# Two more gate chunks as seven products; q and k normed in the recurrence and kept in DRAM; the first branch inside attention

## The chip, the core and the metric

The kernel runs on one core of a Trainium2 chip. The metric is device time in microseconds (us) of one whole execution. The core has a matrix engine, TensorE (PE; its weight loads are listed apart as PEld), and three others: VectorE (DVE), ScalarE (ACT) and GpSimd (POOL). SyncE (SP) issues most DMAs; ACT and POOL issue a few. Each engine runs its instructions in the order of the program and waits on semaphores for what others make.

## The reference

One layer over 1024 frames of width 1024, all in float32:

```
h = RMSNorm(x);  z = h @ w_in -> qa, fa, ia, ga, qb, kb, vb, gate_a, gate_b
oa = HGRN2(qa, fa, ia, ga)           # 4 heads of 128, chunk-causal recurrence
ob = BandAttn(head_rms(qb), head_rms(kb), vb)   # 8 heads of 64, own chunk of 64 and 8 before
x += (sigmoid(gate_a)*(oa @ w_branch_a) + sigmoid(gate_b)*(ob @ w_branch_b)) @ w_out
x += (silu(RMSNorm(x) @ w_gate) * (RMSNorm(x) @ w_up)) @ w_down
x += sigmoid(RMSNorm(x) @ w_ple_gate) * (p @ w_ple_proj)
```

The products hold float32 accuracy: each operand is split into a high part (cast to fp32r) and a rest, and a product of two operands is three matmuls (high by high, high by rest, rest by high).

## The kernel before

**Tiles and names.** A matmul is 128 rows by 128 columns of weights with 512 columns of data, written `128x512`; its result stands in one of eight PSUM banks (`pm`). A weight unit is 128x1024: a raw tile `wr` loaded by SP, its high part `wh` cast on ACT, its rest `wl = wr - wh` made on POOL or DVE. There are two raw tiles (RAW = 2) and four pairs of `wh`, `wl` (RING = 4), so the load of a unit waits until the rest of the unit two before it is made. Large tiles (128x1024) are `s`, small ones `m`; tiles in DRAM are `d`.

**Stages**, by the time in the profiled execution: the first norm and the products for gates, heads and outputs (0 to 284 us); the recurrence of four HGRN heads (about 304 to 437); band attention (447 to 640); the two branches with their gates; the output product; the FFN; the last gate. In the first stage, the table JOBS lists pairs of chunks made as seven half-size products over sums of halves (84 matmuls of 128x512 for a pair instead of 96).

**Recurrence.** `hgrn_mix` of a head begins with two sums over constants, passes levels m = 1, 2, 4, 8, 16, 32, 64 (a few matmuls, then a chain of DVE multiplications and ACT copies that the next level needs), transposes, and ends with eight steps of state. `weave` puts pieces of other work, the fill, between them, by a table of expected durations: the gate chunks of FIRSTS (four, 48 matmuls each), `attn_v`, and the first block of 128 frames of the q/k product. The fill is what PE does while a level's chain runs on DVE and ACT.

**Attention.** `attn_in` makes q and k for two halves of the heads (eight blocks each, four pieces of work per block, six matmuls a piece). A block is squared on ACT, summed on DVE, raised to the power -1/2 on POOL, and scaled on DVE into an SBUF tile. `attention` runs 34 steps; a step takes two pieces from the feed, and has scores, softmax, transposes and the product with v of up to five blocks. Weight rests are made by `rest()` on DVE from a queue, one or two a step, except those that `direct=True` sends to POOL. Late in the loop (steps 23, 25, 27, 28 of SPLITS) the four tiles of oa, loaded back from DRAM, are split into high part and rest on ACT and POOL.

**Branches.** `branches` then makes the eight chunks of the first branch from oa, multiplied by their gates, and the eight of the second from ob.

The helper lines matter when reading rows: L102 is the matmul, L105 the transpose, L97 the DMA that SP issues, L142 the cast of a weight unit, L150 its rest, L72 any other operation recorded through the ordering helper.

## Time and profile before

| | |
|---|---|
| median of three runs | 1539.81 us (1539.76 to 1542.86) |
| the profiled execution | 1538.44 us |
| span in its profile | 1536.7 us |
| mean granted clock of TensorE | 0.998 |
| PE busy | 1512.6 us, 98% of the span |
| DVE, ACT, POOL busy | 1106.7, 661.0, 643.2 us |
| 304.3 to 437 us: PE, DVE, ACT, POOL busy | 128.40, 102.47, 49.41, 19.06 of 132.70 us |
| 447 to 640 us: PE, DVE, ACT, POOL busy | 188.81, 133.22, 136.59, 69.91 of 193.00 us |

Rows of a group give line, engine, operation and tiles, the count, busy time, mean of one in ns, then the idle time of the engine ahead of them and what ended it. A row of the timeline gives the start, the length, and in brackets how long the engine had waited and for what. A row of a window gives its bounds, its length, then for each of PE, PEld, DVE, ACT, POOL the busy time with the count of instructions, then the granted clock, the share of the DMA engines and GB/s.

### The profile page before, as it was taken

The numbers are of one execution on the slowest core, as the hardware profiler recorded it, in microseconds if no ns is written. First come the engines' busy times: TensorE is split into PE (matmuls) and PEld (weight loads), VectorE is DVE, ScalarE is ACT, GpSimd is POOL, SyncE is SP. The second block draws the span as 40 slices with busy tenths as digits, with TensorE's granted clock in tenths as the row PEclk, the third lists the DMA queues.
The fourth block names the chain that finished last, engine by engine and source line by source line (L and its number), as shares of the span: only waits on it lengthen the run. The fifth ranks groups of instructions, "written<-read, shape, count | busy, mean of one in ns | idle before, by whom it ended". The sixth has DMA issues, their size and how long they took to land.

```text
span 1536.7 us, 20687 instructions
## 1 busy us (share of the span) xinstructions
PE 1512.6 (98%) x7692; PEld 1249.2 (81%) x7692; DVE 1106.7 (72%) x1599; ACT 661.0 (43%) x1109; POOL 643.2 (42%) x357
## 2 busy tenths in 40 slices
PE   8999999999999999999999999999999999999998
PEld 6888888888877877888888788888888888888886
DVE  5877776578766768447888877777777667756677
ACT  6633333434347768422575222222222234446452
POOL 4243333101132425254203666665555545545446
PEclk9999999999999999999999999999999999999999
DMA  5552444699553464676345344443333388875335
GB/s 210 189 171 83 144 144 144 219 318 326 179 144 56 98 169 144 189 223 201 123 162 183 114 118 125 123 126 107 103 103 103 103 322 307 282 271 178 124 102 200
DMA packets 97908, 258.66 MB, mean 168 GB/s; under 512 B 10128, under 2 KB 14992, under 8 KB 97296
## 3 DMA queue, kind: packets, MB, share of 16 engines
q1 hardware_dynamic: 91264, 241.60, 45.7%
q0 software_dynamic: 6400, 15.73, 6.1%
q8 instruction: 60, 0.98, 0.3%
q14 instruction: 40, 0.33, 0.1%
q10 hardware_dynamic: 144, 0.02, 0.0%
HBM read 194.13 MB, written 94.63 MB: 188 GB/s over the span
## 4 chain that ended last, share of the span: by engine, by line
PE 89%; DVE 5%; DMA 2%; ACT 2%; issue 1%; POOL 1%; SPq 0%; ACTq 0%; DVEq 0%; POOLq 0%
PE pm L102 86%; DVE s L72 4%; PE pm L105 2%; DMA wr<-in_wv 1%; DVE m L72 0%; ACT s L72 0%; ACT wh L142 0%; ACT m L72 0%; DMA wr<-in_fm 0%; DMA s<-in_x 0%; DVE q L72 0%; POOL m L72 0%; DVE s L337 0%; DVE t L72 0%; ACT t L72 0%
## 5 line engine op out<-in xcount | busy, mean ns | idle before, releaser
L102 PE MATMUL pm<-s,whi 128*128 128x512 f32 x1848 | 569.3, 389 | 0.6 <-DVE t L72 0.6
L102 PE MATMUL pm<-s,wh 128*128 128x512 f32 (+1 forms) x1520 | 472.1, 392 | 7.2 <-ACT wh L142 5.0
L102 PEld LDWEIGHTS pm<-s,whi 128*128 128x128 f32 x1848 | 346.6, 188 | 73.5 <-DVE t L72 1.6
L102 PE MATMUL pm<-s,wlo 128*128 128x512 f32 x924 | 359.5, 389 | 0.0
L102 PEld LDWEIGHTS pm<-s,wh 128*128 128x128 f32 x1520 | 284.3, 189 | 67.4 <-ACT wh L142 5.0
L72 DVE TENSOR_TENSOR s<-s,s 128x512 f32<-128x512 f32 (+3 forms) x236 | 285.6, 1239 | 51.2 <-ACT s L72 38.4
L102 PE MATMUL pm<-s,wl 128*128 128x512 f32 (+1 forms) x760 | 296.1, 390 | 0.5 <-POOL wl L150 0.5
L150 POOL TENSOR_TENSOR wl<-wr,wh 128x1024 fp32r<-128x1024 f32 (+2 forms) x72 | 175.8, 2446 | 220.3 <-ACT wh L142 216.1
L72 DVE TENSOR_TENSOR t<-pm,t 128x512 f32<-128x512 f32 x163 | 112.3, 689 | 139.3 <-PE pm L102 116.8
L102 PEld LDWEIGHTS pm<-s,wlo 128*128 128x128 f32 x924 | 173.5, 188 | 35.9
L142 ACT CAST wh<-wr 128x1024 fp32r<-128x1024 f32 (+2 forms) x104 | 104.5, 1005 | 204.4 <-PE pm L102 81.7
L102 PE MATMUL pm<-wh,s 128*128 128x512 f32 x512 | 180.7, 407 | 0.0
L102 PEld LDWEIGHTS pm<-s,wl 128*128 128x128 f32 x760 | 143.3, 189 | 30.7 <-POOL wl L150 1.2
L72 POOL TENSOR_TENSOR wlo<-q,whi 128x512 fp32r<-128x512 f32 x64 | 102.6, 1604 | 151.9 <-ACT whi L72 81.7
L72 POOL TENSOR_TENSOR wlo<-wr,whi 128x1024 fp32r<-128x1024 f32 (+1 forms) x65 | 136.0, 2098 | 68.8 <-ACT whi L72 59.8
L72 ACT CAST s<-s 128x1024 fp32r<-128x1024 f32 (+1 forms) x98 | 94.5, 983 | 57.8 <-DVE s L72 31.6
L72 ACT CAST whi<-q 128x512 fp32r<-128x512 f32 (+1 forms) x96 | 72.8, 758 | 107.4 <-PE pm L102 87.1
L72 POOL TENSOR_TENSOR m<-m,mhalf 128x8 f32<-128x8 f32 (+1 forms) x24 | 35.1, 1462 | 192.2 <-DVE m L72 192.1
L72 POOL TENSOR_TENSOR s<-t,rb 128x512 f32<-128x512 f32 x44 | 70.7, 1608 | 98.5 <-ACT t L72 98.5
L102 PEld LDWEIGHTS pm<-wh,s 128*128 128x128 f32 x512 | 96.3, 188 | 18.4
L102 PE MATMUL pm<-wl,s 128*128 128x512 f32 x256 | 100.0, 391 | 0.0
L72 ACT ACTIVATE t<-s 128x512 f32<-128x512 f32 x44 | 27.8, 633 | 159.3 <-DVE s L72 155.3
(151 smaller groups left out, 1769.1 us busy)
## 6 DMA issues: line engine op xcount, KB each, us to landing
s<-d SPq DMA_DIRECT2D x83, 512.0 KB, 6.5
d<-s SPq DMA_DIRECT2D x87, 256.0 KB, 2.4
wr<-d SPq DMA_DIRECT2D x36, 512.0 KB, 3.9
d<-s SPq DMA_DIRECT2D x32, 512.0 KB, 4.4
d<-t SPq DMA_DIRECT2D x50, 256.0 KB, 2.5
wr<-in_sz SPq DMA_DIRECT2D x22, 512.0 KB, 6.1
wr<-in_sg SPq DMA_DIRECT2D x22, 512.0 KB, 3.7
wr<-in_su SPq DMA_DIRECT2D x22, 512.0 KB, 4.4
```

Of the source, the lines that this page charges most:

```text
L72: return lambda *a, **k: self.trunk.order(op(*a, **k), self.key)
L102: return self.order(self.nc.tensor.matmul(*a, **k))
L105: return self.order(self.nc.tensor.transpose(*a, **k))
L142: self.nc.scalar.copy(hi[:, c], raw[:, c])
L150: rest.tensor_tensor(lo[:, c], raw[:, c], f32(hi[:, c]), ALU.subtract)
```

## The change

It has five parts.

1. **Gates.** FIRSTS loses chunks 4 and 5; JOBS gains the pair ('gate', 4). PE's 128x512 matmuls fall by 12 in all.
2. **q and k.** The recurrence's fill now ends with the first five blocks of q/k, not one. A block's result is copied out of PSUM (on ACT in the recurrence, on DVE in attention), squared, summed, raised to -1/2, multiplied by that on POOL (`qk_norm`), stored to DRAM, and loaded back one block ahead in attention (`qk_load`). There are 16 stores and 16 loads of 256 KB.
3. **Weight units.** `fetch` issues a unit's load; the cast on ACT and the rest come three ticks of the fill later, and the rest is always on POOL. DVE makes no weight rests in these stages.
4. **First branch.** `branch_a` follows q/k in attention's feed, from step 20; its sources are loaded at step 17 and split at steps 18, 19, 19, 20 on ACT and POOL. A chunk's product is two pieces, the first two sources and then the other two.
5. **Second branch.** Its first two sources are split at steps 28 and 29, the last two in halves at the loop's end; `branches` makes only this branch.

Rows from the order of instructions on one engine follow (tile numbers as the program has them; the line of a helper is one higher after the change). ACT, in the head whose fill casts the q/k weights: before, the fourth head. `s553` is its k, `m618`, `m624`, `m632` the copies that a level's matmuls need, and `wh616`, `wh620`, `wh629` weight units.

```order
L142 CAST wh616_3619<-wr616_3620 128x1024
L72 COPY m618_3636<-s553_3296 128x512
L565 ACTIVATE m621_3655<-pm587_3510,m604_3569 128x128 x4
L142 CAST wh620_3650<-wr620_3651 128x1024
L565 ACTIVATE m622_3660<-pm597_3548,m606_3575 128x128 x4
L72 COPY m624_3671<-s553_3296 128x512
L142 CAST wh629_3704<-wr629_3705 128x1024
L72 COPY m632_3721<-s553_3296 128x512
```

After, the third head (`s499` is its k; `m585`, `m599` are parts of the next head's tiles for the sums; `s441` to `s444` hold v; `wh579` and `wh587` are q/k weights; `s555` is the level's matrix):

```order
L72 COPY m583_3510<-s499_3080 128x512
L72 CAST m585_3517<-m566_3426 128x512
L641 ACTIVATE s441_2805<-pm543_3326,m79_436 128x128
L641 ACTIVATE s442_2806<-pm543_3326,m79_436 128x128
L641 ACTIVATE s443_2807<-pm543_3326,m79_436 128x128
L641 ACTIVATE s444_2808<-pm543_3326,m79_436 128x128
L72 CAST wh579_3481<-wr579_3482 128x1024
L72 CAST m599_3566<-m567_3428 128x512
L524 COPY s555_3374<-pm602_3579 32x8x32
L72 CAST wh587_3527<-wr587_3528 128x1024
```

The q/k weights are cast one head earlier, and now stand behind the casts of the next head's parts and a copy.

POOL where the sources of the first branch are split. Before, late in attention (`s1146`, `s1190`, `s1236` are rests of sources, `m1148`, `m1192` the powers, `wl1202`, `wl1203` weight rests):

```order
L72 TENSOR_TENSOR s1146_5768<-s1111_5635,s1145_5767 128x1024
L72 TENSOR_TENSOR m1148_5779<-m1148_5779,mhalf_100 128x8
L72 DMA d483_2971<-d467_2900 128x1024
L72 TENSOR_TENSOR s1190_5942<-s1112_5637,s1189_5941 128x1024
L72 TENSOR_TENSOR m1192_5953<-m1192_5953,mhalf_100 128x8
L72 TENSOR_TENSOR wl1202_5992<-wr1202_5994,wh1202_5993 128x1024
L72 TENSOR_TENSOR wl1203_5998<-wr1203_6000,wh1203_5999 128x1024
L72 DMA d511_3119<-d502_3060 128x1024
L72 TENSOR_TENSOR s1236_6136<-s1113_5639,s1235_6135 128x1024
```

After (`s1086` to `s1089` are the four rests, `wl1092`, `wl1104`, `wl1112` weights of the branch, `m1105` a power, `m1093` the multiplication of a q/k block):

```order
L72 TENSOR_TENSOR s1086_5579<-s1086_5579,s1103_5629 128x1024
L72 TENSOR_TENSOR m1105_5642<-m1105_5642,mhalf_100 128x8
L72 TENSOR_TENSOR m1093_5603<-m1093_5603,m1105_5642 128x512
L72 DMA d516_3186<-in_wq 256x1x512
L72 TENSOR_TENSOR wl1092_5598<-wr1092_5600,wh1092_5599 128x1024
L72 TENSOR_TENSOR s1087_5581<-s1087_5581,s1123_5706 128x1024
L72 TENSOR_TENSOR s1088_5583<-s1088_5583,s1124_5709 128x1024
L72 TENSOR_TENSOR wl1104_5638<-wr1104_5640,wh1104_5639 128x1024
L72 DMA d493_3070<-in_wq 256x1x512
L72 TENSOR_TENSOR wl1112_5670<-wr1112_5672,wh1112_5671 128x1024
L72 TENSOR_TENSOR s1089_5585<-s1089_5585,s1146_5785 128x1024
```

Rests of sources and of the branch's weights now stand together in POOL's order, five to eight steps earlier in the loop, with a power and a multiplication of q/k among them. PE's first bank of the branch takes `s1086`, `wl1092` and `s1087` in this order, and `s1088`, `s1089` two pieces of the feed later.

POOL where the second half's q/k weights come. Before (`m860` is a power, the `wl` are the four weight rests):

```order
L72 TENSOR_TENSOR m860_4639<-m860_4639,mhalf_100 128x8
L72 TENSOR_TENSOR wl870_4678<-wr870_4680,wh870_4679 128x1024
L72 TENSOR_TENSOR wl882_4724<-wr882_4726,wh882_4725 128x1024
L72 DMA d432_2755<-d422_2687 128x1024
L72 TENSOR_TENSOR wl891_4765<-wr891_4767,wh891_4766 128x1024
L72 TENSOR_TENSOR wl904_4833<-wr904_4835,wh904_4834 128x1024
```

After, in steps 3 to 5 of attention's loop:

```order
L72 TENSOR_TENSOR m768_4301<-m768_4301,mhalf_100 128x8
L72 TENSOR_TENSOR m757_4265<-m757_4265,m768_4301 128x512
L72 DMA d448_2833<-in_oq 256x1x512
L72 TENSOR_TENSOR wl756_4260<-wr756_4262,wh756_4261 128x1024
L72 TENSOR_TENSOR wl767_4297<-wr767_4299,wh767_4298 128x1024
L72 TENSOR_TENSOR wl775_4329<-wr775_4331,wh775_4330 128x1024
L72 TENSOR_TENSOR wl786_4371<-wr786_4373,wh786_4372 128x1024
```

The four rests follow a block's power, multiplication and an accumulating DMA; the load of `wr775` waits for `wl756`, that of `wr786` for `wl767`, as there are two raw tiles.

The diff, cut to its core:

```diff
-SPLITS = (23, 25, 27, 28)
+SPLITS = (18, 19, 19, 20)
...
-FIRST = 4
+FIRST = 5
...
-FIRSTS = (0, 1, 4, 5)
-JOBS = (('gate', 2), ('gate', 6), ('head', 1), ('gate', 8), ('head', 2), ('gate', 10), ('head', 3), ('gate', 12), ('gate', 14), ('out', 0), ('out', 2))
+FIRSTS = (0, 1)
+JOBS = (('gate', 2), ('gate', 4), ('gate', 6), ('head', 1), ('gate', 8), ('head', 2), ('gate', 10), ('head', 3), ('gate', 12), ('gate', 14), ('out', 0), ('out', 2))
...
+    def fetch(self):
+
+        if self.wnext < len(self.worder):
+            hi, lo, raw, ap = self.unit()
+            c = slice(0, ap.shape[1])
+            self.load(raw[:, c], ap[:, c])
+
+            def cast():
+                yield
+                yield
+                self.A.copy(hi[:, c], raw[:, c])
+                self.G.tensor_tensor(lo[:, c], raw[:, c], f32(hi[:, c]), ALU.subtract)
+                self.wready.append((hi, lo))
+
+            self.later.append(cast())
+    def tick(self):
+        for g in list(self.later):
+            if next(g, self) is self:
+                self.later.remove(g)
...
+    def got(self, n=1):
+        while len(self.wready) < n:
+            assert self.later
+            self.tick()
+        got, self.wready = self.wready[:n], self.wready[n:]
+        return got
+
+    def lazy(self, ws):
+        for _ in range(4):
+            ws += self.got()
+            yield ws[-1]
...
     def attn_v(self):
-        ws = self.weights(4, ahead=0, direct=True)
+        self.fetch()
+        ws = []
         self.v = [self.slot() for _ in range(4)]
-        yield 0
         for blks in ((0, 1), (2,), (3,), (4,), (5,), (6, 7)):
             pss = []
-            for j, _ in enumerate(self.tokens(ws, blks, pss)):
+            for j, _ in enumerate(self.tokens(ws or self.lazy(ws), blks, pss)):
                 if blks[0] == 0 and j == 1:
                     self.gate_keep()
-                if blks[0] == 6:
-                    self.weights(0, ahead=(j + 1) // 2, direct=True)
+                if blks[0] == 6 and j % 2:
+                    self.fetch()
...
+    def qk_norm(self, k, ps):
+
+        late = self.stacks
+        qk, sq = [self.small(HALF, tag="qk" if late else "bias", shape=(P, HALF if late else 640))[:, :HALF] for _ in range(2)]
+        (self.V.tensor_copy if late else self.A.copy)(qk, ps)
+        self.A.activation(sq, ps, AF.Square)
+        yield
+        ss = self.small(8)
+        heads = lambda t: t.rearrange("p (a d) -> p a d", d=64)
+        self.V.tensor_reduce(ss, heads(sq), axis=AX.X, op=ALU.add)
+        b = k % 8
+        self.V.tensor_scalar(ss, ss, 1.0 / 64, self.epsv[:, b:b + 1], ALU.mult, ALU.add)
+        self.G.tensor_tensor(ss, ss, self.mhalf[:, 0:8], ALU.pow)
+        self.G.tensor_tensor(heads(qk), heads(qk), ss[:, :].unsqueeze(2).to_broadcast([P, 8, 64]), ALU.mult)
+        yield
+        yield
+        yield
+        self.store(self.qk_at(k), qk)
...
+            ws = []
             for b in range(8):
                 pss = []
-                for n, _ in enumerate(self.tokens(ws, (b,), pss)):
+                for _ in self.tokens(ws or self.lazy(ws), (b,), pss):
                     if b == 7:
-                        self.weights(0, ahead=n + 1 if two == 0 else 2, direct=True)
-                    if n < 3:
-                        yield 1296
-                    if n == 0 and late:
-                        scale()
-                (ps,) = pss
-                sq = self.small(HALF, tag="qk")
-                self.A.activation(sq, ps, AF.Square)
-                ss = self.small(8)
-                self.V.tensor_reduce(ss, sq[:, :].rearrange("p (a d) -> p a d", d=64), axis=AX.X, op=ALU.add)
-                self.V.tensor_scalar(ss, ss, 1.0 / 64, self.epsv[:, b:b + 1], ALU.mult, ALU.add)
-                self.G.tensor_tensor(ss, ss, self.mhalf[:, 0:8], ALU.pow)
-                late.append((two, b, ps, ss))
-                yield 1296
-        scale()
+                        self.fetch()
+                    yield 1296
+                self.later.append(self.qk_norm(8 * two + b, pss[0]))
+
+    def qk_load(self, k):
+        if k < 16:
+            self.qk[k] = self.small(HALF, tag="qk")
+            self.load(self.qk[k], self.qk_at(k))
...
-        feed = self.feed
+        feed = chain(self.feed, self.ticked(self.branch_a()))
...
+            if n % 2 == 0:
+                self.qk_load(n // 2 + 1)
...
+            for _ in range(SPLITS.count(n)):
+                self.osrc.append(self.split_in(raws[len(self.osrc)]))
+            if n in (whole - 4, whole - 3):
+                bsrc.append(self.split_in(braws[len(bsrc)]))
+            if n == whole:
+                bsrc += [(self.slot(F32R), self.slot(F32R)) for _ in range(2)]
+                self.split_half(bsrc, 0)
+            next(feed, None)
...
-            self.rest(False)
-            if n > whole - 5:
-                self.rest(False)
...
+            if n == whole // 2 + 1:
                 self.keep_heads(self.ob, self.obd, [0, 1])
-            if n == whole - 11:
-                raws = self.branch_load(self.od)
-            if n == whole - 4:
-                while self.queue:
-                    self.rest()
-                self.queue = None
-                self.gate_load()
-                self.gate_load()
-                self.branch = self.branches()
-                feed = chain(feed, self.branch)
+                raws = self.load_in(self.od)
+            if n == whole // 2 + 4:
+                for _ in range(2):
+                    self.gate_load()
+            if n == whole - 6:
+                braws = self.load_in(self.obd[:2])
...
+    def split_in(self, raw):
+
+        hi = self.slot(F32R)
+        self.A.copy(hi, f32(raw[:, :]))
+        self.G.tensor_tensor(raw, f32(raw[:, :]), f32(hi[:, :]), ALU.subtract)
+        return hi, raw
...
-        (w,) = self.weights(1)
+        (w,) = self.got()
+        if c:
+            self.fetch()
...
+    def branch_a(self):
+
+        self.m = {}
+        for dd in range(4):
+            (w,) = self.got()
+            next(self.adds, None)
+            if dd:
+                self.fetch()
+            if dd < 2:
+                self.gate_load()
+            for i in range(2):
+                c = 2 * dd + i
+                wh, wl = w
+                todo = [(half, j) for half in range(2) for j in range(2)]
+                if c == 0:
+                    todo.sort(key=lambda t: t[1])
+                pss = {}
+                for half, j in todo:
+                    hs = slice(half * HALF, half * HALF + HALF)
+                    if j == 0:
+                        pss[half] = self.mm()
+                    ps = pss[half]
+                    pairs = self.feature_pairs(w, self.osrc[:2 * j + 2], half, i * HALF)[2 * j:]
+                    drain(self.gemm(ps, pairs, first=j == 0, last=j == 1))
+                    if j:
+                        self.V.tensor_tensor(self.branch_tile(c, half), ps, self.bgates[c][:, hs], ALU.mult)
+                    yield 1296
...
+                fill = self.ticked(chain(*[self.gate_first(c) for c in FIRSTS], self.attn_v(), islice(self.feed, 4 * FIRST)))
```

144 lines of the change are left out of this document (73 added, 71 removed).

## Prediction

> **What bounds the kernel now.** I read the page's busy shares first, then the chain of waits, then one row a stage from the windows, and last the groups of PE's waits.
>
> ```profile
> PE 1512.6 (98%) x7692; PEld 1249.2 (81%) x7692; DVE 1106.7 (72%) x1599; ACT 661.0 (43%) x1109; POOL 643.2 (42%) x357
> ...
> PE 89%; DVE 5%; DMA 2%; ACT 2%; issue 1%; POOL 1%; SPq 0%; ACTq 0%; DVEq 0%; POOLq 0%
> ```
>
> PE sets the end, and only its instructions and the gaps between them count. The windows tell what there is to win: a stretch of seven-product work, the recurrence, attention, and the stretch from attention's end into the branches.
>
> ```profile
> 160.00:200.00 40.00, 40.00 (x178) 33.14 (x177) 30.78 (x38) 12.81 (x19) 16.15 (x10) 1.00 0.44 155
> 304.30:437.00 132.70, 128.40 (x868) 107.48 (x868) 102.47 (x180) 49.41 (x113) 19.06 (x11) 1.00 0.82 268
> 447.00:640.00 193.00, 188.81 (x1495) 152.79 (x1494) 133.22 (x458) 136.59 (x350) 69.91 (x44) 0.99 0.48 117
> 600.00:640.00 40.00, 36.80 (x333) 30.76 (x332) 27.03 (x82) 27.96 (x62) 15.69 (x10) 0.96 0.53 138
> ```
>
> In the first stretch 178 matmuls fill 40.00 us: 0.225 us each, no gap. PE stands idle 4.3 us in the recurrence and 4.2 in attention, 3.2 of these in the last row, where the granted clock is 0.96: (1 - 0.96) x 40 = 1.6 us more. These 8.5 + 1.6 us are all that better cover can win here; new waits have no such limit. In the groups of PE's waits, the first two rows are those of 285 to 440 us, the rest those of 440 to 640:
>
> ```profile
> PE pm L102 <- ACT m L72: 2.3, 4, 1.4
> PE pm L102 <- DVE s L72: 1.7, 2, 1.0
> ```
>
> ```profile
> PE pm L105 <- DVE m L72: 1.3, 2, 1.0
> PE pm L105 <- ACT m L72: 1.2, 1, 1.2
> PE pm L102 <- DVE m L72: 1.0, 1, 1.0
> PE pm L105 <- DVE s L72: 0.7, 1, 0.7
> ```
>
> PE waits nowhere on POOL or on a weight in either list. POOL's groups by form give the prices that the change adds:
>
> ```profile
> L72 POOL TENSOR_TENSOR wl<-wr,wh 128x1024 fp32r<-128x1024 f32 x20 | 48.6, 2437 | 75.0 <-ACT wh L142 73.9 <-issue 1.1
> L72 POOL TENSOR_TENSOR s<-t,rb 128x512 f32<-128x512 f32 x44 | 70.7, 1608 | 98.5 <-ACT t L72 98.5
> L72 POOL TENSOR_TENSOR m<-m,mhalf 128x8 f32<-128x8 f32 x16 | 26.6, 1665 | 84.3 <-DVE m L72 84.2
> L72 POOL DMA_DIRECT2D d<-in_wq x12 | 12.9, 1076 | 3.9 <-issue 3.9
> ```
>
> A rest of 128x1024 holds POOL 2.44 us, a power 1.67, an accumulating DMA 1.08. The new q/k multiplication isn't in the trace; the nearest row, a POOL product of the same size, took 1.61, which I take. A rest is the time of eleven matmuls: PE outruns POOL wherever rests stand in a row.
>
> **The change part by part.** The sum is made against the profiled execution, 1538.4 us, which is 1.4 under the runs' median of 1539.8.
>
> A. *Gates.* Twelve matmuls fewer: 12 x 0.225 = -2.7. The sums that a seven-product pair adds on DVE, ACT and POOL lie under PE in a stage without gaps (DVE busy 30.78 of 40), so nothing for them; without cover, one rest, 2.4.
>
> B. *The first head.* The last v weight is loaded at the same place of SP's order as before:
>
> ```profile
> 319.89 0.33 SPq L97 DMA_DIRECT2D wr<-in_wv  x1
> ```
>
> ```profile
> 326.44 0.71 PE L102 MATMUL pm<-s,wh 128*128 128x512 f32 x2
> 326.54 1.06 ACT L142 CAST wh<-wr 128x1024 fp32r<-128x1024 f32 x1 [2.88 <-DMA wr<-in_wv]
> ```
>
> Its cast waited for the landing and ended at 327.60, and nothing on PE waited, since another gate chunk stood between. That chunk is gone from here, and PE comes to this weight at 326.44: 1.15 us to the cast, then the rest's 2.44 against two matmuls, 0.45, so 2.0. I take +3.2 (0 if the load is ready sooner, to 3.3).
>
> C. *The third head.* The q/k weights are now cast here. The nearest rows are those of the fourth head, which casts them before; PE, ACT, POOL and DVE there:
>
> ```profile
> 417.45 1.13 PE L102 MATMUL pm<-s,m 128*128 128x128 f32 x8 [1.44 <-ACT m L72]
> 426.66 1.13 PE L102 MATMUL pm<-s,m 128*128 128x128 f32 x8 [0.78 <-DVE s L72]
> 432.35 1.12 PE L102 MATMUL pm<-s,s 128*64 128x64 f32 x16 [0.95 <-DVE s L72]
> ```
>
> ```profile
> 416.74 0.62 ACT L72 COPY m<-s 128x512 f32<-128x512 f32 x1 [3.06 <-DVE s L72]
> ```
>
> ```profile
> 413.75 2.40 POOL L72 TENSOR_TENSOR wl<-wr,wh 128x1024 fp32r<-128x1024 f32 x1 [2.75 <-ACT wh L142]
> 419.41 2.82 POOL L72 TENSOR_TENSOR wl<-wr,wh 128x1024 fp32r<-128x1024 f32 x1 [3.26 <-ACT wh L142]
> ```
>
> ```profile
> 418.66 1.32 DVE L72 TENSOR_TENSOR s<-s,s 128x512 f32<-128x512 f32 x2
> 419.90 2.47 DVE L72 TENSOR_TENSOR s<-s 128x128 f32<-128x128 f32 x1
> ```
>
> PE waited 1.44 at a level because DVE's chain was held while POOL made a rest: the 128x128 product at 419.90 took 2.47 us beside the rest at 419.41, while two 128x512 products at 418.66 took 1.32 together. The same is due in the third head: 1.4. Then the casts themselves: `wh579` and `wh587` stand behind the next head's casts, four scalings of v and a copy that waits for DVE, and the first block of q/k wants them in the same head. With a cast at 1.06, a scaling under a third of that (128x128) and a rest at 2.44 against 0.45 of matmuls, PE waits 1.4 for `wl579`, 0.4 and 0.95 for the copy and `wh587`, 2.0 for `wl587`: 6.1 with the level's 1.4. Some of it overlaps: +5 (2 to 6.1).
>
> D. *The fourth head* loses its weight rests, and gets five blocks of q/k as fill: three POOL products of 1.61 instead of rests of 2.44. Its waits above make 3.2; I take -2.5 (-3.2 to 0). What is late next is DVE's chain itself, 102.47 of 132.70 us busy in the recurrence.
>
> E. *Attention, steps 4 and 5.* The second half's four weights are loaded two at a time. Their rests stand in POOL's order behind a power, a multiplication and an add (1.67 + 1.61 + 1.08 = 4.4), and the third load waits for the first rest:
>
> ```profile
> wr<-in_qk SPq DMA_DIRECT2D x6, 512.0 KB, 4.2
> ```
>
> From the end of the first rest: landing 4.2, cast 1.06, rest 2.44: 7.7 us, in which PE has only the pieces of one and a half steps. By the step rows in F I find 2.5 for the first rest, 1.65 for the third weight, 2.0 for its rest: 6.2, of which I take +5 (2.3 to 6.9).
>
> F. *The first branch's start* is the largest term. The rows of before's second half give the pace of a step on PE (scores of three steps, a piece of the feed) and the price of a source's rest on POOL:
>
> ```profile
> 551.29 0.62 PE L102 MATMUL pm<-s,m 64*128 64x256 f32 x6
> 555.21 0.62 PE L102 MATMUL pm<-s,m 64*128 64x256 f32 x6
> 558.37 0.48 PE L102 MATMUL pm<-wh,s 128*128 128x512 f32 x1
> 559.95 0.79 PE L102 MATMUL pm<-s,m 64*128 64x384 f32 x6
> ```
>
> ```profile
> 579.02 2.40 POOL L72 TENSOR_TENSOR s<-s,s 128x1024 fp32r<-128x1024 f32 x1 [6.68 <-ACT s L72]
> ```
>
> Put the first branch's first piece at 558.37. The first source's cast follows step 18's transposes on ACT, so POOL starts about 553.9. In POOL's order there (quoted with the change): first rest to 556.3, power 558.0, multiplication 559.6, add 560.7, the weight's rest to about 563.3 with issue. PE wants it two matmuls in, at 558.8: 4.5 of waiting. The second source's rest ends 565.7, PE has 0.45 of work: 1.95. Then come the third source, two more weight rests, an add, and only then the fourth source, at 576.4; PE, with scores, transposes and the second half's piece between, wants it at 569.85: 6.55. Together 13.0. ACT or DVE may let POOL begin a little sooner: +11 (8 to 15). Behind the waiting matmul stand the next steps' scores, so softmax is late too, but has no work of its own to lose. The price of no cover is this term itself.
>
> G. *Slower clock after waits.* At attention's end in before, three waits close together had this behind them:
>
> ```profile
> 607.31 0.44 PE L105 MATMUL pm<-eye,m 128*128 128x128 f32 x2 [0.97 <-DVE m L72]
> 608.45 0.74 PE L105 MATMUL pm<-eye,s 128*128 128x128 f32 x5 [0.70 <-DVE s L72]
> 609.55 1.30 PE L105 MATMUL pm<-eye,m 128*128 128x128 f32 x5 [0.36 <-DVE m L72]
> 610.56 1.22 PE L102 MATMUL pm<-s,wh 128*128 128x512 f32 x2
> ```
>
> Two matmuls took 1.22 us, 0.71 in B's row; the window puts the loss at 1.6. I add one such loss for F: +1.6 (0 to 3.2). The Trainium skill (TensorE: Matmul & The Clock Gate, "What's actually happening") says that an idle window of some 3.4 us halves the clock until PE has been busy about as long. The rows show the halving after shorter waits, 2.0 us spread over three. By that rule F's two long waits would cost about 1.7 each: an estimate, 3.4 in place of 1.6.
>
> H. *Attention's old waits.* The branch now feeds the late steps, where before had nothing for its second place of a step. The three waits just quoted (2.0) with their slow clock (1.6) should go, and this one probably:
>
> ```profile
> 622.65 0.77 PE L105 MATMUL pm<-eye,m 128*128 128x128 f32 x5 [1.18 <-ACT m L72]
> ```
>
> 2.0 + 1.6 + 1.2 = 4.8; I take -4.5 (-5.8, with the 1.0 on a DVE tile of the list, to -3).
>
> The 16 stores and 16 loads of 256 KB: nothing. SP's queue and the DMA engines are at a share of 0.48 in attention, and a block is loaded two steps ahead; without that cover a late load costs one landing, 4.2 at most. DVE gets a copy per block in place of its scaling, and loses its weight rests.
>
> Sum: -2.7 + 3.2 + 5 - 2.5 + 5 + 11 + 1.6 - 4.5 = +16.1, so 1554.5 profiled and, with 1.4, **1556** by the runs. The ends of all terms give +0.6 to +29; not all fall on one side, so the forecast's own range is 1546 to 1565.
>
> **The rivals.**
>
> *Rests are never last (the other side).* If POOL gets to the four sources and the weights some 13 us sooner than F has it, PE meets them ready. For it: POOL is busy 69.91 of 193 us in attention, and the sources are loaded two steps before. Against: POOL is in order, and the splits stand behind a power that waits for the block's sum. It decides at the first piece of the branch: under 0.5 us of waiting there, and this holds. Then: -2.7, -3.2 in the fourth head, -4.8 and 1.0 in attention: -11.7, and 1528 by the runs.
>
> *Only the branch's start waits, and by half.* B, C and E come to nothing because fill stands elsewhere than I place it; F is 6.5, and D and H hold: -2.7 - 2.5 + 6.5 + 1.6 - 4.5 = -1.6: 1538; with one of C and E left, 1543. I put it at 1541. For it: PE waits on no weight in either list of before. Against: the order rows.
>
> *DVE held by POOL.* Row 419.90 shows a DVE product of two SBUF inputs lengthened from under 0.7 to 2.47 us beside a POOL rest. POOL now also has the q/k multiplications and all rests. Some 25 more POOL instructions of 1.6 to 2.4 us, each holding a DVE instruction for about 0.4 us more than I counted, put 10 us on the softmax chain: 1566. Against: DVE loses rests of its own. The Trainium skill (SBUF — State Buffer, "Who interferes with whom") has the mechanism as an exclusive lock: whichever starts first blocks the other when DVE reads two SBUF inputs. The row agrees, 2.47 us.
>
> That the change doesn't do what it says is excluded by the order: PE has 12 matmuls of 128x512 fewer.
>
> **How the numbers follow.** Forecast 0.60, rests never last 0.15, half 0.15, DVE held 0.10. A measurement of this kernel can tell 0.2%, 3.1 us, from no change: the bounds are 1536.7 and 1542.9. The forecast is slower but for 0.02; the half case parts into 0.03 faster, 0.07 the same, 0.05 slower; the others are on one side. So faster 0.18, same 0.09, slower 0.73. The range 1537 to 1566 leaves out the first rival (0.15) and about half of the last (0.05).
>
> **What would show it.** In the groups of PE's waits for 447 to 640 us, releasers on POOL: `s` (sources) and `wl`, with one wait over 4 us near the branch's first piece, another over 4 at the fourth source, and a granted clock under 0.99 there; near 475 to 490 us waits on `wl` or `wh` of 5 us in sum; near 330 a wait on the v weight of 3 us; in the third head some 5 us on `m`, `wl` and `wh`, and in the fourth under 1. The seven-product stage should end about one pair later, the recurrence start shorter by two chunks. I am wrong if POOL's first source rest starts over 8 us ahead of the branch's first matmul, or if DVE's instructions in attention are longer one by one.

## The result, and the profile after

The changed kernel takes 1566.62 us (median of six runs, 1565.31 to 1570.8) against 1539.54 for the kernel before: a ratio of 1.0176, with a 95% interval of 1.0161 to 1.0191. It is slower, as forecast, but by 27.1 us and not 16.2, and so 0.6 us outside the range of 1537 to 1566. The profiled execution took 1567.15 us, its span is 28.7 us longer than before's.

The page of after, busy shares and chain of waits:

```profile
span 1565.4 us, 20771 instructions
...
PE 1522.9 (97%) x7680; PEld 1253.3 (80%) x7680; DVE 1121.2 (72%) x1595; ACT 664.2 (42%) x1119; POOL 677.9 (43%) x382
...
PE 66%; DVE 4%; DMA 3%; POOL 3%; issue 3%; ACT 1%; SPq 0%; POOLq 0%; ACTq 0%; DVEq 0%
```

PE has the 12 instructions less and is busy 10 us more. So the loss isn't only waiting: its instructions got longer. The windows of after, first by 40 us, then by 5 us within these:

```profile
400.00:440.00 40.00, 34.34 (x218) 28.20 (x218) 27.78 (x45) 15.50 (x34) 13.63 (x8) 0.91 0.57 168
...
480.00:520.00 40.00, 34.91 (x218) 25.81 (x219) 25.23 (x83) 25.76 (x75) 24.69 (x16) 0.91 0.60 160
...
560.00:600.00 40.00, 33.96 (x256) 26.99 (x255) 20.99 (x76) 22.78 (x63) 14.56 (x11) 0.92 0.63 194
600.00:640.00 40.00, 32.45 (x193) 23.63 (x193) 30.19 (x67) 22.74 (x58) 22.65 (x14) 0.82 0.91 268
```

```profile
495.00:500.00 5.00, 3.71 (x12) 2.33 (x12) 4.31 (x2) 0.17 (x1) 3.55 (x2) 0.50 0.90 211
...
595.00:600.00 5.00, 3.93 (x13) 3.25 (x14) 1.46 (x7) 2.69 (x6) 4.92 (x5) 0.50 0.46 170
...
615.00:620.00 5.00, 3.36 (x15) 1.90 (x16) 4.96 (x5) 2.72 (x8) 5.00 (x3) 0.50 1.03 356
```

The granted clock isn't a little lower: it is 0.50 in whole stretches, and 1.00 outside of them. In windows of 0.1 us it falls at 419.7, 494.8, 593.8, 604.1 and 610.9 us and rises at 426.5, 501.6, 600.5, 607.4 and 621.1. All of these lie whole multiples of 3.41 us apart, to within 0.1, so in this profile the clock changes on a grid of that length; one low interval of it costs at most half, 1.7 us of work. Taken in windows of 1 us from 285 to 760 us, busy time times (1 - clock) sums to 13.1 us, against 1.6 in before. PE's waits, by group, in the recurrence (285 to 440 us; the first two rows), then in attention and the branches (440 to 660):

```profile
PE pm L103 <- POOL wl L72: 4.3, 3, 2.4
PE pm L103 <- ACT m L72: 1.6, 2, 1.5
```

```profile
PE pm L103 <- ACT m L72: 5.5, 3, 4.6
PE pm L103 <- POOL wl L72: 5.1, 3, 3.7
PE pm L106 <- DVE s L72: 3.6, 1, 3.6
PE pm L103 <- POOL s L72: 3.2, 2, 1.6
PE pm L106 <- DMA m<-d: 1.4, 1, 1.4
```

All waits over 0.1 us between 285 and 760 us are 27.23 us, against 9.47 in before. So 17.8 more of waits and 11.5 more at half clock make 29.3; the work itself (the rest of the time up to the output product) fell by 1.4, not 2.7. The sum, 27.9, is what the start of the output product moved (728.0 to 755.9); the stages behind it hold the last 0.8. The places of the waits, in PE's timeline of after:

```profile
347.59 0.50 PE L103 MATMUL pm<-wl,s 128*128 128x512 f32 x1 [1.35 <-POOL wl L72]
...
402.39 1.13 PE L103 MATMUL pm<-s,m 128*128 128x128 f32 x8 [1.48 <-ACT m L72]
...
421.38 0.79 PE L103 MATMUL pm<-wl,s 128*128 128x512 f32 x1 [2.36 <-POOL wl L72]
...
496.29 0.79 PE L103 MATMUL pm<-wl,s 128*128 128x512 f32 x1 [3.66 <-POOL wl L72]
...
593.94 0.70 PE L103 MATMUL pm<-m,s 128*64 128x128 f32 x4 [4.62 <-ACT m L72]
596.07 0.69 PE L106 MATMUL pm<-eye,m 128*128 128x128 f32 x2 [1.43 <-DMA m<-d]
...
603.66 0.52 PE L103 MATMUL pm<-s,wh 128*128 128x512 f32 x1 [1.58 <-POOL s L72]
...
611.95 0.66 PE L106 MATMUL pm<-eye,s 128*128 128x128 f32 x2 [3.60 <-DVE s L72]
...
617.01 0.79 PE L103 MATMUL pm<-s,wh 128*128 128x512 f32 x1 [1.64 <-POOL s L72]
```

At the first branch's start, five waits make 12.9 us, and who is late differs from wait to wait. What ACT, DVE and POOL do there:

```profile
591.54 1.04 ACT L72 CAST s<-s 128x1024 fp32r<-128x1024 f32 x1 [4.99 <-DMA s<-d]
...
597.31 1.04 ACT L72 CAST wh<-wr 128x1024 fp32r<-128x1024 f32 x1 [3.00 <-DMA wr<-in_ba]
```

```profile
603.52 8.28 DVE L72 TENSOR_SCALAR s<-s,m 128x256 f32<-128x256 f32 x1
```

```profile
600.77 5.15 POOL L72 TENSOR_TENSOR s<-s,s 128x1024 fp32r<-128x1024 f32 x2
605.42 2.82 POOL L72 TENSOR_TENSOR wl<-wr,wh 128x1024 fp32r<-128x1024 f32 x1
607.74 1.52 POOL L72 DMA_DIRECT2D d<-in_wq  x1
608.34 3.30 POOL L72 TENSOR_TENSOR wl<-wr,wh 128x1024 fp32r<-128x1024 f32 x1
```

ACT stood 4.99 us at the first source's cast for its landing, with the exponentials and copies of attention behind it: that is PE's 4.62. DVE's scaling of a softmax began at 603.5 and ended at 611.8, when POOL's row of rests did (611.6): that is PE's 3.60. In before each of the four scalings of this form took 0.35 us, as in the first row here; the second and third are DVE and POOL of after, where two weight rests stood in a row:

```profile
462.12 0.35 DVE L72 TENSOR_SCALAR s<-s,m 128x256 f32<-128x256 f32 x1
```

```profile
494.73 3.98 DVE L72 TENSOR_SCALAR s<-s,m 128x256 f32<-128x256 f32 x1
```

```profile
493.40 5.15 POOL L72 TENSOR_TENSOR wl<-wr,wh 128x1024 fp32r<-128x1024 f32 x2
```

That scaling too ended (498.7) just after the rests (498.6). Only the waits on `s` and `wl` are the queue on POOL of which the prediction spoke.

### The profile page after: what moved, and what is told of

It is laid out like the page before. It is cut to its first block, busy times and chain, and to the rows that moved or that the text cites. A ratio compares the mean times of both kernels' runs of the same rounds, so it can differ in the third digit from the quotient of the medians.

```text
span 1565.4 us, 20771 instructions
## 1 busy us (share of the span) xinstructions
PE 1522.9 (97%) x7680; PEld 1253.3 (80%) x7680; DVE 1121.2 (72%) x1595; ACT 664.2 (42%) x1119; POOL 677.9 (43%) x382
## 4 chain that ended last, share of the span: by engine, by line
PE 66%; DVE 4%; DMA 3%; POOL 3%; issue 3%; ACT 1%; SPq 0%; POOLq 0%; ACTq 0%; DVEq 0%
PE pm L103 64%; DVE s L72 3%; PE pm L106 2%; DMA s<-d 1%; DMA d<-in_oq 1%; POOL wl L72 1%; POOL m L72 1%; POOL s L72 0%; POOL wl L151 0%; DMA wr<-in_wv 0%; DVE q L72 0%; DVE m L72 0%; POOL d L72 0%; DMA wr<-in_qk 0%; ACT wh L72 0%
## 5 line engine op out<-in xcount | busy, mean ns | idle before, releaser
L103 PE MATMUL pm<-s,whi 128*128 128x512 f32 x1904 | 586.4, 389 | 0.6 <-DVE t L72 0.6
L103 PE MATMUL pm<-s,wh 128*128 128x512 f32 (+1 forms) x1456 | 455.6, 394 | 10.6 <-ACT wh L143 5.2
L103 PEld LDWEIGHTS pm<-s,whi 128*128 128x128 f32 x1904 | 357.1, 188 | 75.4 <-DVE t L72 1.7
L103 PE MATMUL pm<-s,wlo 128*128 128x512 f32 x952 | 370.4, 389 | 0.0
L103 PEld LDWEIGHTS pm<-s,wh 128*128 128x128 f32 x1456 | 272.4, 189 | 69.9 <-ACT wh L143 5.2
L103 PE MATMUL pm<-s,wl 128*128 128x512 f32 (+1 forms) x728 | 284.8, 391 | 1.0 <-POOL wl L151 0.5
L103 PEld LDWEIGHTS pm<-s,wlo 128*128 128x128 f32 x952 | 178.7, 188 | 37.5
L103 PEld LDWEIGHTS pm<-s,wl 128*128 128x128 f32 x728 | 137.5, 189 | 30.3 <-POOL wl L151 1.2
L143 ACT CAST wh<-wr 128x1024 fp32r<-128x1024 f32 (+3 forms) x81 | 80.1, 991 | 163.6 <-DMA wr<-d 47.6
L72 POOL TENSOR_TENSOR wl<-wr,wh 128x1024 fp32r<-128x1024 f32 x25 | 62.8, 2534 | 83.7 <-ACT wh L72 71.7
```

The source lines that it names most:

```text
L72: return lambda *a, **k: self.trunk.order(op(*a, **k), self.key)
L103: return self.order(self.nc.tensor.matmul(*a, **k))
L143: self.nc.scalar.copy(hi[:, c], raw[:, c])
```

## The experiments

The time of the kernel before is 1538.7 to 1540.5 us in all of them; ratios are to it. Waits are sums of those over 0.1 us between 285 and 760 us in the profiled execution, "at half clock" is the sum of the section above in the same execution, which need not be the median one.

### The first branch taken out of attention

```diff
-        feed = chain(self.feed, self.ticked(self.branch_a()))
+        feed = chain(self.feed, self.ticked(0 for _ in range(12)))
...
-        self.bsrc, self.feed = bsrc, feed
+        self.bsrc, self.feed = bsrc, self.ticked(self.branch_a())
```

> The changed kernel with the first branch taken out of attention's feed: its products run after attention's last step, sources and weights are loaded and split where the change has them. Theory A (from the trace of after: at the branch's start ACT stands behind a source's cast whose load lands late, DVE behind a scaling held by a row of POOL rests, and the clock is at half after each long wait): the waits between 590 and 618 us (13.6 us) and the half clock there (7.7 us of work lost) go, and the old waits at attention's end come back (3 to 5 us): 1547 to 1551 us. Theory B (the prediction's step: POOL's queue is last there): the same, 1546 to 1552. Rival C (DVE is held by POOL all through attention): not below 1560.

1584.32 us, ratio 1.0291 (1.0271 to 1.0310): slower than the changed kernel by 18 us, against both theories. The sources are still split at steps 18 to 20, and with no matmuls of the branch to run beside, the burst of rests does worse. PE and DVE of this kernel:

```profile
608.83 0.66 PE L106 MATMUL pm<-eye,s 128*128 128x128 f32 x2 [9.55 <-DVE s L72]
```

```profile
601.59 7.10 DVE L72 TENSOR_SCALAR s<-s,m 128x256 f32<-128x256 f32 x1
```

The DVE scaling is held again, 7.10 us, beside a row of POOL rests (four of them, 598.8 to 608.5). From 614 to 670 every step or two waits 0.3 to 2.3 us for DVE or ACT: with q/k done by step 19, attention alone doesn't fill PE. Waits are 39.8 us in all, 17.2 more are lost at half clock. So the branch in attention is cover that the moved q/k blocks leave wanting; taking it out doesn't cure how it begins.

### Sources loaded sooner, and their rests moved to DVE

Three kernels: the four sources loaded one at a time at steps 9, 11, 13, 15; their rests on DVE; both.

```diff
+            if n in (9, 11, 13, 15):
+                raws += self.load_in([self.od[len(raws)]])
...
-                raws = self.load_in(self.od)
```

```diff
-                self.osrc.append(self.split_in(raws[len(self.osrc)]))
+                self.osrc.append(self.split_in(raws[len(self.osrc)], self.V))
...
-        self.G.tensor_tensor(raw, f32(raw[:, :]), f32(hi[:, :]), ALU.subtract)
+        (rest or self.G).tensor_tensor(raw, f32(raw[:, :]), f32(hi[:, :]), ALU.subtract)
```

> The changed kernel with the four sources of the first branch loaded one at a time at steps 9, 11, 13, 15 instead of all at step 17; splits unchanged. Theory A: ACT no longer waits 4.99 us for the first source's landing; PE's waits of 4.62 on ACT and 1.43 on a q/k load go with one stretch of half clock (2.5): about 1558 us. Theory B (POOL's queue is last): POOL and PE both come sooner, the wait returns as a wait on POOL's rests (13.0 by the prediction's rows against 13.6 now): 1564 to 1568. Rival C: no change, 1566.

> The changed kernel with the rests of the first branch's four sources on DVE instead of POOL; loads unchanged at step 17. Theory A: the late landing stays (PE waits 4.6 on ACT, 1.4 on the q/k load), but the waits on source rests (3.2) and most of the 3.6 us on DVE's held scaling go, with about 4 us of half clock: 1556 to 1558 us. Theory B: POOL keeps only weight rests: of 13.0 about 11 go: 1551 to 1554. Rival C (DVE is the bound in attention): slower than now, over 1568.

> Both edits: sources loaded one at a time at steps 9 to 15, and their rests on DVE. Theory A: the terms add, since one is ACT behind a DMA and the other DVE and POOL: 13 us of waits and 7 of half clock mostly gone: 1546 to 1550 us. Theory B: the early load adds nothing to the other edit: 1551 to 1554. Rival C: over 1560.

| kernel | us | ratio (interval) | waits | at half clock |
|---|---|---|---|---|
| changed | 1566.62 | 1.0176 (1.0161 to 1.0191) | 27.2 | 13.1 |
| sooner | 1562.98 | 1.0147 (1.0132 to 1.0162) | 23.6 | 12.1 |
| rests on DVE | 1561.21 | 1.0140 (1.0120 to 1.0161) | 24.7 | 9.0 |
| both | 1554.11 | 1.0091 (1.0076 to 1.0106) | 19.7 | 6.3 |

The early load takes the waits of 4.62 and 1.43 away (0.36 is left), and in their place stands this, in PE's timeline of that kernel:

```profile
596.05 0.50 PE L103 MATMUL pm<-s,wl 128*128 128x512 f32 x1 [3.34 <-POOL wl L72]
```

That is the first of the prediction's three waits on POOL, hidden in the changed kernel behind a later one. So neither theory holds alone: the landing was last, POOL's queue was next behind it. The first two times lie outside what either theory gave, and the third just outside B's (by 0.1), while B's reason, that the early load adds nothing, fails: it takes 7.1 us off the kernel with rests on DVE. With both edits 12.5 us go, more than the 3.6 and 5.4 of the two apart, which is what two causes at one place do. What DVE takes for a rest, in the kernel with both:

```profile
586.09 1.22 DVE L72 TENSOR_TENSOR s<-s,s 128x1024 fp32r<-128x1024 f32 x1 [0.32 <-ACT s L72]
...
592.87 6.04 DVE L72 TENSOR_TENSOR s<-s,s 128x1024 fp32r<-128x1024 f32 x2 [0.32 <-ACT s L72]
```

1.22 us alone, 3.0 each beside two POOL rests. The softmax scaling that took 8.28 us in the changed kernel took 9.38 with the sources sooner and their rests on POOL, and 0.35 with these on DVE.

### Weight rests on DVE, and loads of gates parted

On top of both edits, the lagging weights' rests go to DVE too; and then two of the four gate loads of step 20 go to step 22.

```diff
-                self.G.tensor_tensor(lo[:, c], raw[:, c], f32(hi[:, c]), ALU.subtract)
+                self.V.tensor_tensor(lo[:, c], raw[:, c], f32(hi[:, c]), ALU.subtract)
```

> Third edit on top of early_dve (1554.1 us): the rests of the lagging weight units too are made on DVE, not on POOL. There PE still waits 11.1 us on such rests (0.76, 0.60, 2.37, 3.65, 0.95, 2.74) with some 5 us of half clock. Theory D (a rest of 2.4 us on POOL against 0.45 us of matmuls is what is late; on DVE one took 1.22 us alone): each wait shrinks by about 1.2, and the half clock by half: 1544 to 1548 us. Rival E (the weight comes late already, by its load or cast, or DVE's own chain is in the way): waits move to the DVE rows, 1552 to 1558.

> wdve with the loads of four gate tiles parted: two tiles at step 20, two at step 22, not four at step 20. In early_dve a q/k load issued with them landed late and PE waited 1.14 us for it. If the burst is the cause, that wait goes: 1 to 1.5 us under wdve. If not: as wdve.

1553.41 us (1.0093, 1.0078 to 1.0108) and 1554.97 (1.0103, 1.0087 to 1.0118): no gain from either. PE's timeline of the first of them:

```profile
345.33 0.98 PE L103 MATMUL pm<-s,s 128*64 128x64 f32 x7 [2.76 <-DVE s L72]
...
502.02 0.93 PE L103 MATMUL pm<-m,s 128*64 128x128 f32 x8 [3.54 <-ACT m L72]
```

The waits on `wl` shrank as theory D said (3.65 to 0.76 in attention), but others came, as rival E said: on the level chain, which is DVE's work, and on ACT's copies. A faster engine for the rests alone gains nothing, as it is late with its own work instead. The wait on a q/k load that parting the gates was to remove (1.14) was gone in the first of the two already, so the burst's part in it stays untested.

### Casts without the lag

```diff
             def cast():
-                yield
-                yield
+                yield from ()
```

> The changed kernel with the casts of the fetched weights at the first tick after the load instead of the third. Theory D (the lag isn't what costs; rests on POOL are): ACT, in order, now stands behind landings of 4 to 11 us at each unit, and PE waits for ACT's copies: slower than 1566.6, 1570 to 1585. Rival F (the lag makes the weights late in the third head and at steps 4 and 5: 4.2 and 5.1 us of waits with half clock behind them): 1556 to 1562.

1575.68 us, ratio 1.0238 (1.0221 to 1.0255), with 34.8 us of waits. ACT, then PE, in this kernel:

```profile
597.52 1.04 ACT L72 CAST wh<-wr 128x1024 fp32r<-128x1024 f32 x1 [10.38 <-DMA wr<-in_ba]
```

```profile
599.14 1.23 PE L103 MATMUL pm<-s,m 64*128 64x256 f32 x6 [9.64 <-ACT m L72]
```

A cast ahead of its landing holds all that ACT has behind it. The lag, all told, isn't what costs; it saves 9 us.

### The price of a wait

The kernel before, with eight made waits in the stage without gaps; the result of the added instructions is not used.

```diff
+    def stall(self, k):
+        ps, w = self.mm(), self.pause
+        self.tr(ps[:, :P], self.eye, self.eye)
+        self.A.copy(w, ps[:, :P])
+        for _ in range(k):
+            self.G.tensor_tensor(w, w, w, ALU.mult)
+        self.tr(ps[:, P:2 * P], w, self.eye)
```

> The kernel before, with eight made waits of PE in the dense seven-product stage, 19 us apart: PE transposes a tile, ACT copies it, POOL multiplies it 0, 2, 4, 6, 8, 10, 3 and 7 times, and PE's next instruction reads it. It prices a wait. Theory G (the clock halves after some 3 us of idling and stays so until PE has been busy a while): waits under 2 us cost themselves alone; those over 3 to 4 us have a stretch of granted clock 0.50 behind them, which costs about 2.5 to 3.5 us more whatever the wait's length. Rival H (the loss grows with the wait): a short wait has a short stretch of 0.50, a long one a long stretch.

1606.41 us (one execution), 67.7 more: 49.5 of waits, 16.4 at half clock, and 16 transposes. The waits came out longer than planned, as ACT and POOL had other work in their queues. PE's rows of two of them and the windows behind these:

```profile
144.32 0.48 PE L106 MATMUL pm<-eye,pause 128*128 128x128 f32 x1 [4.59 <-POOL pause L73]
...
230.24 0.48 PE L106 MATMUL pm<-eye,pause 128*128 128x128 f32 x1 [8.14 <-POOL pause L73]
```

```profile
144.00:150.00 6.00, 5.68 (x14) 4.53 (x15) 0.01 (x1) 0.05 (x1) 0.26 (x1) 0.50 0.04 13
...
231.00:235.00 4.00, 4.00 (x11) 3.13 (x10) 0.00 (x0) 0.00 (x0) 0.00 (x0) 0.50 0.43 170
```

| wait | 2.73 | 4.59 | 5.76 | 6.24 | 6.50 | 7.18 | 8.14 | 8.40 |
|---|---|---|---|---|---|---|---|---|
| lost at half clock behind it | 0 | 2.8 | 2.5 | 2.3 | 1.9 | 1.6 | 2.5 | 2.8 |

From 4.59 us on the loss is 1.6 to 2.8 us and doesn't grow with the wait, as theory G says, if less than the 2.5 to 3.5 it gave: PE goes on at half clock for 3.3 to 5.7 us after it is back at work. The Trainium skill (TensorE: Matmul & The Clock Gate, "What's actually happening") gives this rule, half clock after an idle window until a busy one. The made waits agree: behind the one of 4.59 the clock stood at 0.50 from 143.2 to 150.0, twice 3.4 us. But PE need not idle throughout: in before, waits of 0.97, 0.70 and 0.36 us close together, with work between, had 0.50 behind them from 609.4 to 612.7. How much idling is enough isn't settled here.

### Two blocks to a weight

If weights come late because the ring of four pairs frees a pair only three or four pieces ahead of the next unit's use, then two blocks that share each weight, at both ends of a half of q/k, give three pieces more.

```diff
-            for b in range(8):
+            for blks in [(0, 1), (2,), (3,), (4,), (5,), (6, 7)]:
...
-                    if b == 7:
+                    if blks[-1] == 7 and j % 2:
                         self.fetch()
...
+                for b, ps in zip(blks, pss):
+                    self.later.append(self.qk_norm(8 * two + b, ps, 5 * (b - blks[0])))
```

> The changed kernel with two blocks of frames made together at both ends of each half of q/k (blocks 0 and 1, blocks 6 and 7: a weight unit serves both before the next unit is taken; the second block's norm starts five ticks later). Between the release of a tile pair in the weights' ring and the first use of the unit loaded into it there are then some three pieces of the feed more, 4 us. Theory D (a weight comes late because the ring frees its tiles only three or four pieces ahead of its use, and load 4 to 8 us, cast 1.06 and rest 2.44 do not fit): the waits on weights in the third head (4.2 us) and at steps 4 and 5 (4.6) go with two stretches of half clock (5.0): 1553 to 1558 us. Rival E (they are late by their place in the queues of ACT and POOL): unchanged, 1564 to 1568.

> The same with early_dve's edits (sources loaded one at a time at steps 9 to 15, their rests on DVE; alone 1554.1). Theory D: the gains add: 1541 to 1546 us. Rival E: 1553 to 1556.

> As two_early, but the first two sources are loaded at steps 7 and 9 and split at steps 12 and 14, and only the last two are loaded at step 17 and split at 19 and 20. If the burst of copies, rests and landings around step 18 is what remains there, it is halved: 2 to 4 us under two_early. If the last two sources' late landing now holds ACT as in the changed kernel: 3 to 6 over it.

> early_dve's kernel with that order of loads and splits alone (no blocks made together). Against early_dve's 1554.1: 2 to 4 us less if the burst is the cause, 3 to 6 more if the late landing of the last two sources holds ACT.

| kernel | us | ratio (interval) | waits | at half clock |
|---|---|---|---|---|
| two blocks | 1553.39 | 1.0096 (1.0079 to 1.0113) | 18.2 | 6.3 |
| and sources sooner, rests on DVE | 1543.68 | 1.0024 (1.0014 to 1.0035) | 11.9 | 1.7 |
| two sources at 7, 9, split at 12, 14 | 1543.85 | 1.0025 (1.0012 to 1.0039) | | |
| that order, no shared weights | 1559.53 | 1.0126 (1.0111 to 1.0141) | 23.0 | 11.9 |

Theory D's forecasts hold. Sharing alone brings 13.2 us: the 3.7 us on weights in the third head and the 4.6 at steps 4 and 5 are gone, with the half clock behind them, while a wait on DVE in that head grew from 0.50 to 1.39. Rival E, the place in the queues, falls, for casts and rests stand on the same engines in the same order. One thing isn't parted: sharing also gives PE twelve matmuls to a weight in place of six, and so each next rest more time; how much of the gain is the ring's earlier release and how much this, no run tells. The other order of loads brings nothing with sharing and costs 5.4 without. There it isn't the sources that PE waits for, but q/k blocks whose loads landed late:

```profile
594.32 0.69 PE L106 MATMUL pm<-eye,m 128*128 128x128 f32 x2 [2.88 <-DMA m<-d]
...
624.86 0.66 PE L106 MATMUL pm<-eye,m 128*128 128x128 f32 x2 [2.86 <-DMA m<-d]
```

(The waits of the third kernel are left out: its executions lie between 1542.3 and 1549.2, and the profiled one is the longest.)

### What was left

The kernel at 1543.68 still had these in PE's, ACT's and DVE's timelines:

```profile
475.44 1.12 PE L103 MATMUL pm<-s,m 64*128 64x128 f32 x6 [1.54 <-ACT m L72]
```

```profile
474.27 0.60 ACT L72 ACTIVATE m<-pm 128x512 f32<-128x512 f32 x1 [5.54 <-DMA d<-m]
```

```profile
398.73 3.17 DVE L72 TENSOR_TENSOR s<-s,s 128x512 f32<-128x512 f32 x2
```

ACT waited for a store to free a tile, and two DVE products of the level chain took 3.17 us (1.28 a row before) beside one POOL rest. Five edits followed, each on the one ahead but where said: a fifth tile; rests in halves; and on these, casts a tick later, the splits a step sooner, and both.

```diff
-MIXER = {"s": 3, "pt": 4, "bias": 4, "qk": 4, "qs": 2, "state": 2}
+MIXER = {"s": 3, "pt": 4, "bias": 4, "qk": 5, "qs": 2, "state": 2}
```

```diff
-                self.G.tensor_tensor(lo[:, c], raw[:, c], f32(hi[:, c]), ALU.subtract)
+                for x in range(0, ap.shape[1], HALF):
+                    h = slice(x, x + HALF)
+                    self.G.tensor_tensor(lo[:, h], raw[:, h], f32(hi[:, h]), ALU.subtract)
```

```diff
-SPLITS = (18, 19, 19, 20)
+SPLITS = (18, 18, 19, 19)
```

> two_early with five tiles in place of four for the q/k norm's copies. There ACT stood 5.54 us at attention's start for the store of an earlier block to free a tile, and PE 1.54 us behind it, with 1.7 us of work lost at half clock. If the tile is the cause, both go: 1540 to 1541 us. If the wait only moves (the PSUM bank or the next store): 1543 to 1544.

> qk5 with each weight rest of the lagging units made in two halves of 512 columns on POOL (one took 1.6 us where the whole took 2.44). PE uses the first half first, and DVE can slip between the halves. If POOL's hold on DVE is what makes PE wait in the recurrence (1.34, 1.48, 1.39), these waits shrink by 0.7 each: 1538 to 1539.5. If POOL's time counts (3.2 against 2.44 a unit): no gain over qk5, or 1 to 2 us worse.

> qk5_halves (1539.6 us) with casts at the fourth tick after the load instead of the third. If ACT standing behind a landing is the rest of the loss at attention's start, PE's 1.05 and 0.66 us there go: 1537.5 to 1538.5. If a later cast makes weights late elsewhere (third head, first branch): 1541 to 1545.

> qk5_halves with the four sources split at steps 18, 18, 19, 19 (the last one and the second one step sooner). If the last source is late by its step: PE's waits between 586 and 594 us (0.2, 0.45, 0.76, 0.3) fall by 1 to 1.5: 1538 to 1538.6. If two splits in one step hold DVE or ACT: 1540 to 1543.

> Both: 1536 to 1537.5 if both latenesses are what is left, and so 2 to 3 us under the kernel before; over 1540 if the placement has its own cost.

| kernel | us | ratio (interval) | waits | at half clock |
|---|---|---|---|---|
| fifth tile | 1539.70 | 1.0003 (0.9995 to 1.0012) | 12.6 | 0 |
| and rests in halves | 1539.59 | 0.9999 (0.9990 to 1.0008) | 10.6 | 0 |
| and casts a tick later | 1546.38 | 1.0043 (1.0031 to 1.0055) | 16.1 | 4.8 |
| or splits sooner | 1537.23 | 0.9984 (0.9976 to 0.9993) | 10.3 | 0 |
| or both | 1543.58 | 1.0024 (1.0016 to 1.0033) | 13.0 | 4.4 |

The tile brought 4.0 us by the medians, though the wait moved: the sum of waits rose from 11.9 to 12.6, with 2.39 us on DVE at 483, and the half clock went. The two profiled executions (1540.33 and 1539.44) differ by 0.9 only, which is about what these sums explain; the rest of the 4.0 isn't accounted for. Halves changed nothing that can be told; the expectation's price of 1.6 us a half was wrong, as two took 2.51 us together at their quickest. A later cast makes weights late (2.67 us in the first head). The splits a step sooner give the fastest kernel, 1537.23 us: 2.1 under the kernel before (by the ratio 0.16%, interval 0.07 to 0.24%), 29 under the changed one. The windows of this kernel, to set against the changed one's:

```profile
285.00:440.00 155.00, 150.87 (x916) 126.58 (x915) 106.06 (x174) 61.08 (x128) 40.12 (x30) 1.00 0.76 248
440.00:640.00 200.00, 194.56 (x1506) 156.31 (x1505) 142.14 (x461) 132.13 (x339) 88.97 (x71) 1.00 0.69 186
```

## Why the prediction was wrong in its size

The sign, and where PE would wait, were right. By its own terms, in us, measured in the profile of after:

| step | predicted | measured | |
|---|---|---|---|
| A, gates | -2.7 | -1.4 | work left over without waits and half clock; 12 instructions fewer, as said |
| B, first head | +3.2 | +1.35 | the cast was in time; the wait is on the rest alone, at 347.59 |
| C, third head | +5 | +5.7 | 1.48 at a level, then 0.60, 0.50, 0.72, 2.36 |
| D, fourth head | -2.5 | -2.8 | 3.46 of waits became 0.67 |
| E, steps 4 and 5 | +5 | +5.1 | 0.45, 3.66, 0.98; the parts were not as forecast: 3.66 where 2.5 stood for the first rest, 0.98 where 3.65 stood for the third weight and its rest |
| F, branch's start | +11 | +13.6 | the sum by rows was 13.0 |
| G and H, clock | 0 | +11.5 | +1.6 in G for the branch, -1.6 in H for the old place |
| H, old waits | -2.9 | -4.2 | 0.98, 0.97, 0.70, 0.36, 1.18 are gone |
| sum | +16.1 | +28.8 | with -1.0 of small waits in the first two heads and +0.8 behind the output product's start 28.6; the span: +28.7 |

**The step that failed is G.** It added one loss of clock, +1.6 with 3.2 at most, for F alone, at the size that before's trace shows once. But the terms C and E are rows of waits too, and F is several: the clock went to 0.50 at 420, 495, 594, 604 and 611 us, with 13.1 us lost, 5.3 of them at C and E, which G had at nothing. The trace of before had the evidence in the row that was quoted, and the rule quoted beside it had the right mechanism; both were applied to one place and not to every wait that the sum foresaw. With 2.3 us (the mean of the seven made waits) for the five places, both known only afterwards, G would have been +11.5 and the sum 1566. The prediction's estimate by the Trainium skill (TensorE: Matmul & The Clock Gate, "What's actually happening"), 1.7 a wait for F's two, made 3.4: too little for the same reason.

**F had its size for a wrong reason.** It followed POOL's queue and took the loads as landed, since they are issued two steps ahead of the branch. ACT's queue was not followed to its head: the cast of a source that lands 9 us after its issue, in a burst of two stores and six loads, stands ahead of softmax. 4.62 of the 13.6 us are that, 1.43 are a q/k block's load in the same burst, 3.6 are DVE held by POOL, and 3.7 are waits on POOL's rests. The kernel with the early load shows that POOL's queue was next, with 3.34, 1.57 and 1.64 us where the forecast has 4.5, 1.95 and 6.55: its chain was real, but not last, and too long. (The q/k multiplication, taken at 1.61, took 1.04.) That 11 came near 13.6 is luck.

**The rival "DVE held by POOL"** was priced over the whole of attention, at 0.4 us an instruction. In the profile of after five scalings in attention have it: 3.98, 1.19, 8.28, 2.12 and 2.32 us, where the medians of the same forms in before are 0.35, 0.35, 0.35, 0.23 and 0.42. That is 16 us on DVE, of which PE waited 3.6. In the kernel with shared weights two products of the recurrence took 1.9 us longer at 398.7. It is a mechanism of single places, and that this rival's time, 1566, is the measured one is luck. "Rests never last" and "half" are refuted by the waits. Of the predicted signs, the weights' 5 us at 475 to 505 and the third head's 5 us were found; waits over 4 us on POOL were found neither at the branch's first piece (0.47 and 1.58) nor at the fourth source (1.64). POOL's first source rest started 7.2 us ahead of the branch's first matmul (592.67 and 599.82), near the 8 that would have spoken against F.

**H and D** were right: attention's second half has no wait over 0.1 us from 618 us on until the output product.

What stays open: why A's 2.7 us arrive as 1.4. The branch's pieces alternate with attention's smaller matmuls, which they did not before; that this costs the difference was not tried.

## What to carry to other kernels

Price a forecast wait of PE at its length and, where it is long or one of several close together, at some 2 to 3 us of half clock on top (here 1.6 to 3.6 a stretch); then make the sum over all such places. When work is moved under other work, look at what the first instruction of it waits for on each in-order queue: a cast ahead of its landing stops an engine for everybody, and a row of rests on POOL holds a DVE instruction for the whole row. Where a ring of tiles sets how early a load can start, more work between release and use (here two blocks that share each weight) bought 13 us that neither a faster engine nor another order of casts did.

## What the runs showed of the hardware

A DVE scaling of 128x256 took 8.28 us, where the same form took 0.35 undisturbed, and ended within 0.2 us of POOL's row of rests; others took 3.98 beside a row of two and 7.10 beside the row of the first experiment, and ended within 0.2 us of these. By these three, it doesn't get in between two rests; that POOL's row is the cause is shown by the two kernels with sources sooner, 9.38 us with their rests on POOL and 0.35 with these on DVE. The Trainium skill (SBUF — State Buffer, "Who interferes with whom") has one instruction block the other for its length; here it was the row's length. The length of a wait alone doesn't decide on the clock: one of 2.73 us left it at 1.00, one of 1.54 (at 475.44) had a stretch of 0.50 from 476.0 to 479.4 behind it. And POOL took 2.51 us at its quickest for two rests of 128x512, about as long as for one of 128x1024 (2.40 to 2.44), so that parting them costs next to nothing.
